# Triangular inverses of the third mixer: from elementwise steps with trips through DRAM to products of 32x32 blocks

## The chip, the core and the metric

The kernel runs on one core of a Trainium2 chip. The metric is the time of one execution on the device, in microseconds (us). TensorE (PE in the rows, PEld for its weight loads) multiplies matrices into PSUM, VectorE (DVE), ScalarE (ACT) and GpSimd (POOL) work elementwise, and SyncE (SP) holds the queue in which nearly all transfers of this kernel are issued. Each engine works through its own instructions in the order of the program and waits on semaphores for the others.

## What is computed

A two-layer diffusion backbone over 512 latent and 256 context tokens of 1024 features. Each layer: a modulated norm, one wide input projection, three token mixers (A: gated linear attention, B: windowed attention, C: bidirectional RWKV-7), a gated merge, and a feed-forward block. The change is in mixer C. Its recurrence, for each of 8 heads of 64 values and for both directions, is

```
def step(S, inp):
    w_t, k_t, v_t, kk_t, a_t = inp[:5]
    sa = jnp.einsum('bhvk,bhk->bhv', S, kk_t)
    S = S * w_t[:, :, None, :] - sa[..., None] * (kk_t * a_t)[:, :, None, :] + v_t[..., None] * k_t[:, :, None, :]
    ...
    return S, jnp.einsum('bhvk,bhk->bhv', S, inp[5])
```

The kernel does it in chunks of 32 tokens. Inside a chunk the tokens' updates depend on one another through a strictly triangular 32x32 matrix L, and T = (I + L)^-1 turns that into one product. For 128 tokens of one direction there are 32 such matrices (4 chunks of 8 heads).

## The kernel before

Mixer C (class Rwkv) takes the 768 tokens in six pieces of 128, in each of two directions, "f" and "b": 12 pieces in a layer, 24 in all. For each piece two steps go ahead of the recurrence, together called a front here. `prep` loads decays (cp), replacement vectors and keys (bk) and keys with queries (kr), and makes the scores X (products xp) and transposed keys bkt (products tp). `inverse` makes TT, the 32 inverses. Then `chain` goes through the piece's four chunks, one after the other, since each needs the state S (sblkf, sblkb) that the last one left. A chunk is a row of short products with a copy behind each: yp, its copy ysb on ACT, up (which reads TT), its copies uv on DVE and ACT, sp, and a sum on DVE into S; op and its copy ys make the output. A tail per piece follows (norm, gate).

`run` moves one lane for each direction in turn, a step at a time. While the chain of one piece goes on, two steps of the next front are written between two steps of the chain (`lane`). In layer 0 one front stands ahead of the chain, in layer 1 two. Between the steps `layer` puts projection jobs of other work (24 in a layer: products px of 512 columns and, in layer 0, pz of 256, each with weights raw that ACT and DVE split into wh and wl). In layer 0 the jobs are spread evenly over the steps; in layer 1 `paced` lets 150 products go first and then 3.3 for each product group of the chain. A scheduler then sets the final order on each engine. The PSUM tiles of xp, tp and of the tail have one tag, "a", with two buffers.

Before the change `inverse` works in a layout of its own, where each of the 32 matrices lies along the free axis of four partitions. X goes to DRAM (d1), comes back as L, spread over four partitions each; G starts as the identity, loaded from the input gid; then 31 steps of a product (L1532, into ftmp) and a subtraction (L1533, into G) solve for the inverse, on DVE for "f" and on POOL for "b"; G goes to DRAM (d2) and comes back as TT. That is 62 elementwise instructions and six transfers for a front. `inverse` yields five times, so a front has ten steps.

## Time and profile before

| what | us |
|---|---|
| median of three runs | 3357.53 (3356.67 to 3370.26) |
| profiled execution: span from first to last instruction | 3361.6 |
| stage of mixer C in layer 0 (first decays scanned at 650.9, last state product at 1159) | about 509 |
| stage of mixer C in layer 1 (2397.4 to 2867.9) | about 471 |
| TensorE busy, whole span | 3033.8 (90%) |

The page gives no time of the profiled execution beside its span. The span is 4 us over the median of the runs, so differences that are worked out against it carry over as they are. Starts and windows are counted from the span's start. [...]

### The profile page before, as it was taken

The page shows a single profiled execution, that of the slowest core. Times are in us where ns is not written, and L with a number is a line of the kernel's source. Part 1 is how long each engine was busy: PE and PEld are TensorE (multiplying, and loading weights), DVE is VectorE, ACT ScalarE, POOL GpSimd, SP SyncE. Part 2 cuts the span into 40 slices and gives each one's busy share as a digit, 9 for nine tenths or more (in the row PEclk, how much of TensorE's full clock was granted, in tenths as well). Part 3 has the DMA queues.
Part 4 walks back from the last instruction along what each step waited for, and adds up shares of the span by engine and source line. Part 5 has one row for each costly group of instructions (what it writes and reads, how often), then busy time and mean ns, then how long its engine had stood idle before and what let it go on. Part 6 is the DMA issues. An engine that isn't in the chain of part 4 may idle for free. (4 is left out here: it accounts for less than half of the span.)

```text
span 3361.6 us, 62705 instructions
## 1 busy us (share of the span) xinstructions
PE 3033.8 (90%) x25760; PEld 2400.0 (71%) x25760; DVE 1756.6 (52%) x3506; ACT 1081.2 (32%) x2034; POOL 990.4 (29%) x1438
## 2 busy tenths in 40 slices
PE   6999999878889989999999899698857789799998
PEld 3777877666666778888888787576635466788887
DVE  3175557766656755222223454656567566643335
ACT  3255444422222233212122344453322222332223
POOL 2033122344655322101001211312266465221102
PEclk9999999888888999999999899798868679899999
DMA  7421222544345552443212322123633444512223
GB/s 289 153 74 56 96 101 95 174 131 124 99 119 142 168 197 73 153 157 132 63 63 95 96 73 95 58 76 126 205 103 107 112 131 137 187 69 95 96 98 119
DMA packets 269375, 398.33 MB, mean 118 GB/s; under 512 B 94624, under 2 KB 179360, under 8 KB 269088
## 3 DMA queue, kind: packets, MB, share of 16 engines
q1 hardware_dynamic: 249184, 370.20, 34.2%
q10 hardware_dynamic: 19904, 24.12, 2.0%
q8 instruction: 202, 3.31, 0.4%
q14 instruction: 85, 0.70, 0.1%
HBM read 320.33 MB, written 73.92 MB: 117 GB/s over the span
## 5 line engine op out<-in xcount | busy, mean ns | idle before, releaser
L50 PE MATMUL px<-hh,wl 128*128 128x512 f32 x1584 | 646.5, 408 | 31.9 <-DVE wl L72 31.8
L50 PE MATMUL px<-hh,wh 128*128 128x512 f32 x1584 | 651.9, 412 | 14.1 <-ACT wh L71 6.5
L50 PE MATMUL px<-hl,wh 128*128 128x512 f32 x1584 | 643.2, 406 | 11.6 <-POOL hl L302 8.8
L72 DVE TENSOR_TENSOR wl<-raw,wh 128x1024 fp32r<-128x1024 f32 (+1 forms) x314 | 402.3, 1282 | 366.4 <-ACT wh L71 332.1
L71 ACT ACTIVATE wh<-raw 128x1024 fp32r<-128x1024 f32 (+1 forms) x314 | 326.1, 1041 | 778.8 <-PE pz L50 395.2
L50 PEld LDWEIGHTS px<-hh,wl 128*128 128x128 f32 x1584 | 308.2, 195 | 110.0 <-DVE wl L72 38.1
L50 PEld LDWEIGHTS px<-hh,wh 128*128 128x128 f32 x1584 | 309.4, 195 | 106.7 <-issue 24.4
L50 PEld LDWEIGHTS px<-hl,wh 128*128 128x128 f32 x1584 | 308.8, 195 | 82.3 <-POOL hl L302 13.2
L673 POOL TENSOR_TENSOR al<-fs,ah 128x768 fp32r<-128x768 f32 (+1 forms) x44 | 85.0, 1931 | 726.3 <-ACT ah L672 726.3
L50 PE MATMUL pz<-hl,wh 128*128 128x256 f32 x872 | 253.1, 291 | 3.8 <-DVE hl L304 2.0
L50 PE MATMUL pz<-hh,wh 128*128 128x256 f32 x872 | 253.5, 292 | 1.5 <-DVE fs L663 1.4
L50 PE MATMUL pz<-hh,wl 128*128 128x256 f32 x872 | 252.0, 289 | 1.3 <-DVE wl L72 0.8
L50 PEld LDWEIGHTS pz<-hl,wh 128*128 128x128 f32 x872 | 171.2, 196 | 10.4 <-POOL hl L302 2.6
L50 PEld LDWEIGHTS pz<-hh,wh 128*128 128x128 f32 x872 | 170.3, 196 | 11.2 <-issue 3.2
L50 PE MATMUL px<-y,wh 128*128 128x512 f32 (+1 forms) x512 | 155.8, 391 | 24.8 <-ACT y L123 10.0
L50 PEld LDWEIGHTS pz<-hh,wl 128*128 128x128 f32 x872 | 170.4, 195 | 7.0 <-issue 5.2
L1532 POOL TENSOR_TENSOR ftmp<-G,L 128x60 f32<-128x60 f32 (+24 forms) x372 | 125.9, 338 | 146.9 <-DMA G<-gid 55.8
L1532 DVE TENSOR_TENSOR ftmp<-G,L 128x60 f32<-128x60 f32 (+24 forms) x372 | 107.4, 289 | 103.8 <-DMA G<-gid 55.6
L1533 POOL TENSOR_TENSOR G<-G,ftmp 128x60 f32<-128x60 f32 (+24 forms) x372 | 131.4, 353 | 25.2
L50 PE MATMUL sp<-uv,bkt 64*64 64x64 f32 x1536 | 99.8, 249 | 36.9 <-DVE uv L1593 36.5
L50 PEld LDWEIGHTS px<-y,wh 128*128 128x128 f32 x512 | 96.1, 209 | 44.2 <-ACT y L123 12.5
L50 PEld LDWEIGHTS sp<-uv,bkt 64*64 64x64 f32 x1536 | 69.3, 147 | 75.4 <-DVE uv L1593 41.1
(443 smaller groups left out, 6090.9 us busy)
## 6 DMA issues: line engine op xcount, KB each, us to landing
raw<-win SPq DMA_DIRECT2D x114, 512.0 KB
raw<-w SPq DMA_DIRECT2D x104, 512.0 KB
araw<-wada SPq DMA_DIRECT2D x96, 512.0 KB
raw<-w SPq DMA_DIRECT2D x48, 448.0 KB
kr<-krd SPq DMA_DIRECT2D x24, 512.0 KB
L<-d SPq DMA_DIRECT2D x24, 512.0 KB
gs<-gat ACTq DMA_DIRECT2D x24, 384.0 KB
raw<-wab SPq DMA_DIRECT2D x16, 512.0 KB
```

The source lines that it names most:

```text
L50: return self.nc.tensor.matmul(out, lhsT=lhsT, rhs=rhs, start=start, stop=stop)
L71: nc.scalar.activation(h[:, :n], raw[:, :n], AF.Copy)
L72: nc.vector.tensor_tensor(out=lo[:, :n], in0=raw[:, :n], in1=h[:, :n].bitcast(F32), op=ALU.subtract)
L673: nc.gpsimd.tensor_tensor(out=al, in0=s, in1=ah.bitcast(F32), op=ALU.subtract)
L1532: eng.tensor_tensor(out=t, in0=G[:, rows, j:j + 1].to_broadcast([128, a, m]), in1=L[:, j:j + 1, cols].to_broadcast([128, a, m]), op=ALU.mult)
L1533: eng.tensor_tensor(out=G[:, rows, cols], in0=G[:, rows, cols], in1=t, op=ALU.subtract)
```

## The change

`inverse` stays in the layout of X. Products with the identity take the blocks out of X twice, as they are and transposed, each block to a 32x32 place of its own (tile iu: rows 32 p for head pair p). VT holds two things per matrix, side by side: the inverse so far and its transpose, beginning with blocks of two rows, I minus the masked part of L. Then four rounds double the block size, 2 to 4 to 8 to 16 to 32: Um is the part of L that joins two blocks (a mask product on POOL), pp = Um times the inverse (tile ip), copied to Ps on ACT, and dd = the inverse times that (tile id, for both halves of VT, in the last round for one), which DVE subtracts from VT, in the last round into TT. All transfers of `inverse` go. It yields ten times now, so a front has fifteen steps. Two constants, imask and eye32, are loaded in place of gid. The PSUM tiles iu, ip and id have the tag "a" too. Comments and docstrings are left out of the changed file, which shifts its line numbers.

```diff
         self.masks = ld("rmask", [128, 2, 64], I["rmask"])
+        self.imask = ld("imask", [128, 5, 32], I["imask"])
+        self.eye = ld("eye32", [128, 32], I["eye32"])
...
     def inverse(self, d, g):
-        """T = (I + L)^-1 of 32 blocks (4 chunks x 8 heads), four partitions per block (row mod 4)"""
-        nc, T = self.nc, self.T
-        d1 = self.D.tile([2, 16, 32, 32], F32, name="d1", tag="d1", bufs=3)   # q, (e w p), j, i
-        d2 = self.D.tile([8, 4, 32, 32], F32, name="d2", tag="d2", bufs=3)    # (q e w), p, j, i
+
+
+        nc, K, T, ps = self.nc, self.K, self.T, self.ps
+        MM = nc.tensor.matmul
         X = self.hs[d, g]["X"]
+        R = (slice(0, 32), slice(96, 128))
+        P = [slice(32 * p, 32 * p + 32) for p in range(4)]
+
+        src = [ps.tile([128, 2, 4, 32], F32, name="iu", tag="a", bufs=2) for _ in range(2)]
+        for p in range(4):
+            for e in range(2):
+                for w in range(2):
+                    for q in range(2):
+                        K.mm(src[q][P[p], 0, 2 * e + w, :], X[R[q], e, w, p, 0:32], K.ident[R[q], R[q]])
+        for p in range(4):
+            for q in range(2):
+                K.mm(src[q][P[p], 1].rearrange("r (e w) i -> r e w i", w=2), K.ident[R[q], R[q]], X[R[q], :, :, p, 0:32])
+        VT = T.tile([128, 2, 8, 32], F32, name="VT", tag="VT", bufs=2)
+        Uc = T.tile([128, 8, 32], F32, name="Uc", tag="Uc", bufs=2)
         for q in range(2):
-            r0 = 0 if q == 0 else 96
-            nc.sync.dma_start(d1[q].rearrange("u j i -> j u i"), X[r0:r0 + 32].rearrange("j e w p i -> j (e w p) i")[:, :, 0:32])
-        L = T.tile([128, 32, 32], F32, name="L", tag="L", bufs=2)
-        nc.sync.dma_start(L.rearrange("u j i -> u (j i)"), d1.rearrange("q u j i -> (q u) (j i)").unsqueeze(0).to_broadcast([4, 32, 1024]))
+            b = slice(4 * q, 4 * q + 4)
+            nc.vector.tensor_tensor(out=VT[:, :, b, :], in0=src[q], in1=self.imask[:, 0:1, :].unsqueeze(1).to_broadcast([128, 2, 4, 32]), op=ALU.mult)
+            nc.scalar.copy(Uc[:, b, :], src[q][:, 1])
         yield
-        G = T.tile([128, 8, 32], F32, name="G", tag="G", bufs=2)
-        nc.sync.dma_start(G, self.I["gid"])
-        tmp = T.tile([128, 128], F32, name="ftmp", tag="ftmp", bufs=2)
-        eng = nc.vector if d == "f" else nc.gpsimd
-        for n in range(31):
-            if d == "f":
-                j, rows, cols = n, slice(0, n // 4 + 1), slice(n + 1, 32)
+        flat = VT.rearrange("r t m i -> r (t m) i")
+        nc.gpsimd.tensor_tensor(out=flat, in0=self.eye.unsqueeze(1).to_broadcast([128, 16, 32]), in1=flat, op=ALU.subtract)
+        def part(n):
+            Um = T.tile([128, 8, 32], F32, name="Um", tag="Um" + d, bufs=1)
+            nc.gpsimd.tensor_tensor(out=Um, in0=Uc, in1=self.imask[:, n + 1:n + 2, :].to_broadcast([128, 8, 32]), op=ALU.mult)
+            return Um
+        Um = part(0)
+        yield
+        for n in range(4):
+            last = n == 3
+            pp = ps.tile([128, 8, 32], F32, name="ip", tag="a", bufs=2)
+            for m in range(8):
+                for r in P:
+                    K.mm(pp[r, m, :], Um[r, m, :], VT[r, 0, m, :])
+            Ps = T.tile([128, 8, 32], F32, name="Ps", tag="Ps", bufs=2)
+            nc.scalar.copy(Ps, pp)
+            if not last:
+                Um = part(n + 1)
+            yield
+            dd = ps.tile([128, 2, 8, 32], F32, name="id", tag="a", bufs=2)
+            for m in range(8):
+                for t in (1,) if last else (0, 1):
+                    for r in P:
+                        lw, rh = (Ps, VT[:, 1]) if t else (VT[:, 1], Ps)
+                        K.mm(dd[r, t, m, :], lw[r, m, :], rh[r, m, :])
+            if last:
+                TT = self.hs[d, g]["TT"] = T.tile([128, 8, 32], F32, name="TT", tag="TT", bufs=4 if self.zout else 6)
+                nc.vector.tensor_tensor(out=TT, in0=VT[:, 1], in1=dd[:, 1], op=ALU.subtract)
             else:
-                j = 31 - n
-                rows, cols = slice(j // 4, 8), slice(0, j)
-            a, m = rows.stop - rows.start, cols.stop - cols.start
-            t = tmp[:, 0:a * m].rearrange("q (a b) -> q a b", b=m)
-            eng.tensor_tensor(out=t, in0=G[:, rows, j:j + 1].to_broadcast([128, a, m]), in1=L[:, j:j + 1, cols].to_broadcast([128, a, m]), op=ALU.mult)
-            eng.tensor_tensor(out=G[:, rows, cols], in0=G[:, rows, cols], in1=t, op=ALU.subtract)
-            if n % 8 == 7:
-                yield
-        nc.sync.dma_start(d2.rearrange("m p (a s) i -> s (m p) a i", s=4), G)
-        TT = self.hs[d, g]["TT"] = T.tile([128, 8, 32], F32, name="TT", tag="TT", bufs=4 if self.zout else 6)
-        nc.sync.dma_start(TT, d2.rearrange("m p r i -> (p r) m i"))
-        yield
+                nc.vector.tensor_tensor(out=flat, in0=flat, in1=dd.rearrange("r t m i -> r (t m) i"), op=ALU.subtract)
+            yield
...
-    g = np.zeros((128, 8, 32), f)
-    for s_ in range(4):
-        for a in range(8):
-            g[32 * s_:32 * s_ + 32, a, 4 * a + s_] = 1
-    C["gid"] = g
...
+    r_, c_ = (p % 32)[:, None], np.arange(32)[None, :]
+    C["imask"] = np.stack([((r_ // (2 * n) == c_ // (2 * n)) & (r_ // n != c_ // n)).astype(f) for n in (1, 2, 4, 8, 16)], 1)
+    C["eye32"] = (r_ == c_).astype(f)
```

How the instructions stand on the engines, at three places. First DVE, layer 0, in the midst of a chain. Before, the steps of an inverse (ftmp, G) stand between the chain's copies uv and state sums sblkb, and the first of them waits for a load:

```order
L1533 TENSOR_TENSOR G<-G,ftmp 128x8x2
L1532 TENSOR_TENSOR ftmp<-G,L 128x8
L1533 TENSOR_TENSOR G<-G,ftmp 128x8
L1606 TENSOR_TENSOR sblkb<-sp,scb 64x4x64 x2
L1532 TENSOR_TENSOR ftmp<-G,L 128x31
L1533 TENSOR_TENSOR G<-G,ftmp 128x31
L1593 COPY uv<-up 32x128
L1532 TENSOR_TENSOR ftmp<-G,L 128x30
L1533 TENSOR_TENSOR G<-G,ftmp 128x30
L1593 COPY uv<-up 32x128
```

Now, at a like place, the round's subtractions (VT from id) stand between the same kinds of chain instruction:

```order
L1564 TENSOR_TENSOR VT<-VT,id 128x512
L1619 COPY uv<-up 32x128 x2
L1632 TENSOR_TENSOR sblkb<-sp,scb 64x4x64 x2
L1475 COPY pc<-cp 128x16
L1564 TENSOR_TENSOR VT<-VT,id 128x512 x3
L1619 COPY uv<-up 32x128
L72 TENSOR_TENSOR wl<-raw,wh 128x1024
L1619 COPY uv<-up 32x128
```

Sixty-two short instructions that hang on two loads have become two masked copies, three subtractions and one last one, which hang on TensorE. Second, TensorE, layer 0, in the midst of a chain. Before, projection products stand between the chain's groups:

```order
L1584 MATMUL up<-ysb,TT 32x64 x3
L1564 MATMUL yp<-uv,X 32x64 x8
L50 MATMUL px<-hh_131,wh 128x512
L50 MATMUL px<-hl_139,wh 128x512
L50 MATMUL pz<-hh_131,wh 128x256
L50 MATMUL pz<-hl_139,wh 128x256
L1590 MATMUL op<-sblkb,kr 32x128 x4
L50 MATMUL px<-hh_131,wl 128x512
```

Now rounds of the next front's inverse stand there as well (ip of 32 products, id of 64, of which the first two rows are shown; a product here is one of the program, and each float32 product of these short ones shows as two MATMUL rows in the profile):

```order
L1610 MATMUL up<-ysb,TT 32x64 x5
L1616 MATMUL op<-sblkb,kr 32x128 x4
L1590 MATMUL yp<-uv,X 32x64 x8
L1595 MATMUL yp<-sblkf,kr 32x128 x4
L50 MATMUL px<-hh_134,wh 128x512
L50 MATMUL ip<-VT,Um 32x32 x32
L50 MATMUL sp<-uv,bkt 64x64 x8
L1637 MATMUL op<-uv,X 32x64 x8
L50 MATMUL id<-Ps,VT 32x32 x4
L50 MATMUL id<-VT,Ps 32x32 x4
```

The chain's sp and op have moved behind a group of 32 inverse products, and the id that needs ScalarE's copy of ip follows after 16 short products. Third, SP's queue in layer 0. Before, the transfers of the inverses (d, L, G, TT) stand between the loads of prep (bk, cp, kr), the chain's values (uv) and the weights (raw):

```order
L1516 DMA d_7183<-X 32x16x32 x2
L1518 DMA L<-d_7148 128x1x1024
L1536 DMA d_6578<-G 4x256x32
L1460 DMA bk<-bkdf_3850 128x4x256
L66 DMA raw<-win 128x1024
L1460 DMA bk<-bkdb_3851 128x4x256
L1538 DMA TT<-d_6578 128x8x32
L1521 DMA G<-gid 128x256
L1518 DMA L<-d_7183 128x1x1024
L1536 DMA d_6584<-G 4x256x32
```

Now the same place holds only the others:

```order
L1462 DMA bk<-bkdf_3850 128x4x256
L66 DMA raw<-win 128x1024
L1462 DMA bk<-bkdb_3851 128x4x256
L1579 DMA uv<-vtok_3854 64x512 x2
L66 DMA raw<-win 128x1024
L1461 DMA cp<-twdb_3849 128x4x136
L1463 DMA kr<-krd_3847 128x4x256
```

No load or store of a front waits in SP's queue for an engine's result any more.

## Rows read from the trace of the kernel before

**Rows 1.** The page: busy time by engine; granted clock in 40 slices.
```profile
PE 3033.8 (90%) x25760; PEld 2400.0 (71%) x25760; DVE 1756.6 (52%) x3506; ACT 1081.2 (32%) x2034; POOL 990.4 (29%) x1438
...
PEclk9999999888888999999999899798868679899999
```
**Rows 2.** Windows: length, PE, PEld, DVE, ACT, POOL busy, PEclk, DMA share, GB/s.
```profile
650.00:740.00 90.00, 73.30 (x708) 60.11 (x706) 55.71 (x108) 26.09 (x44) 42.02 (x88) 0.89 0.60 175
740.00:1079.00 339.00, 292.14 (x4097) 212.25 (x4094) 206.55 (x566) 84.49 (x218) 183.47 (x409) 0.85 0.43 120
1079.00:1159.00 80.00, 78.67 (x1043) 59.34 (x1043) 53.05 (x110) 18.08 (x50) 34.38 (x43) 0.98 0.42 129
2397.00:2505.00 108.00, 68.60 (x649) 51.51 (x648) 56.08 (x120) 26.23 (x42) 47.70 (x90) 0.75 0.56 161
2505.00:2743.00 238.00, 186.17 (x2392) 123.86 (x2390) 153.14 (x415) 56.66 (x138) 142.33 (x329) 0.74 0.43 117
2743.00:2868.00 125.00, 124.34 (x1880) 83.35 (x1881) 76.95 (x193) 32.49 (x97) 61.99 (x114) 0.90 0.39 122
```
**Rows 3.** Waits of PE, 650 to 1159: total us, times, longest.
```profile
PE sp L50 <- DVE uv L1593: 31.6, 7, 8.7
PE px L50 <- DVE wl L72: 11.6, 9, 6.7
```
**Rows 4.** Waits of PE, 2397 to 2868: total us, times, longest.
```profile
PE up L1584 <- DMA TT<-d: 27.4, 4, 16.2
PE px L50 <- DVE wl L72: 19.0, 7, 10.8
PE xp L50 <- POOL kr L1479: 11.9, 2, 7.3
```
**Rows 5.** DVE groups, 650 to 1159: busy, mean ns | idle before, releasers.
```profile
L1532 DVE TENSOR_TENSOR ftmp<-G,L 128x60 f32<-128x60 f32 (+24 forms) x186 | 54.1, 291 | 46.1 <-DMA L<-d 23.0 <-DMA G<-gid 12.6 <-issue 5.7
L1533 DVE TENSOR_TENSOR G<-G,ftmp 128x60 f32<-128x60 f32 (+24 forms) x186 | 53.5, 288 | 5.1
```
**Rows 6.** Timeline of DVE near 2502: start, us, what, [idle before <-releaser].
```profile
2502.33 0.19 DVE L1532 TENSOR_TENSOR ftmp<-G,L 128x31 f32<-128x31 f32 x1 [21.02 <-DMA G<-gid]
...
2503.11 0.27 DVE L1593 COPY uv<-up 32x128 f32<-32x128 f32 x1
```
**Rows 7.** The page's groups: inverse steps on both engines, and the product reading TT.
```profile
L1532 POOL TENSOR_TENSOR ftmp<-G,L 128x60 f32<-128x60 f32 (+24 forms) x372 | 125.9, 338 | 146.9 <-DMA G<-gid 55.8
L1532 DVE TENSOR_TENSOR ftmp<-G,L 128x60 f32<-128x60 f32 (+24 forms) x372 | 107.4, 289 | 103.8 <-DMA G<-gid 55.6
...
L1584 PE MATMUL up<-ysb,TT 32*32 32x64 f32 x1536 | 55.7, 245 | 36.1 <-DMA TT<-d 31.0 <-ACT ysb L1574 5.0
```
**Rows 8.** Timeline of PE near 205.7, mixer A: short products in a dense run.
```profile
205.75 1.02 PE L50 MATMUL gsc<-gD,gD 64*32 64x32 f32 x96
206.71 0.87 PE L880 MATMUL gktp<-ident,gkh 128*128 128x128 f32 x6
```
**Rows 9.** Timeline of PE near 519.4: products that all write one column strip.
```profile
519.41 1.68 PE L1412 MATMUL pb<-rksel,kt 128*32 128x2 f32 x48
521.02 0.65 PE L1143 MATMUL sop<-sPT,svt 128*64 128x256 f32 x4
```
**Rows 10.** Timeline of PE near 859.4: 128-column products into four strips.
```profile
859.42 0.43 PE L1590 MATMUL op<-sblkb,kr 128*32 128x128 f32 x8
859.77 0.68 PE L50 MATMUL sp<-uv,bkt 64*64 64x64 f32 x16
```
**Rows 11.** Timeline of PE near 2861, the same form at the lower clock.
```profile
2861.12 0.66 PE L1569 MATMUL yp<-sblkb,kr 128*32 128x128 f32 x8
2861.71 1.18 PE L1584 MATMUL up<-ysb,TT 32*32 32x64 f32 x32
```
**Rows 12.** Windows, columns as in group 2: the end of layer 1's chain.
```profile
2857.50:2868.00 10.50, 10.11 (x184) 6.33 (x167) 4.95 (x12) 2.41 (x10) 2.46 (x4) 0.50 0.14 44
```
**Rows 13.** Instructions on X: the masked copy, duration ns min/median/max.
```profile
L1492 DVE TENSOR_TENSOR X<-xp,rmask x48: 406/680/692, 665.9 to 2728.3; 128x512 f32<-128x512 f32 x40, 128x256 f32<-128x256 f32 x8
```

## The prediction, made before the changed kernel ran

> **What bounds the kernel now.** I read the page first. TensorE is busy for 90% of the span, and its granted clock dips in two stretches, around slices 8 to 14 and 29 to 34 [rows 1]. Those are the two stages of mixer C, so the windows come next [rows 2]. The stage of layer 0 is 509 us long (90 + 339 + 80) with TensorE busy for 444.1, so it idles 64.9; that of layer 1 is 471 us with 379.1 busy and 91.9 idle. DVE and POOL are below 70% in each. What the reader is to see: in these stages TensorE is the fullest engine, what is left to gain are 157 us of its idle time and the time lost to the lower clock, and work added to it has no other place to go. The clock share, weighted by length, is (90 x 0.89 + 339 x 0.85 + 80 x 0.98) / 509 = 0.88 in layer 0 and (108 x 0.75 + 238 x 0.74 + 125 x 0.90) / 471 = 0.785 in layer 1. [...]

> Then the waits of TensorE. In layer 0 half of the idle time is sp waiting for DVE's copy uv, 31.6 us in 7 waits, and 11.6 are for split weights wl [rows 3]. In layer 1 it is up waiting for TT, 27.4, then wl, 19.0, and the scores waiting for POOL's kr, 11.9 [rows 4]. The groups of DVE say why a copy of 0.27 us is late by up to 8.7: the first step of an inverse stands in DVE's order and waits for its loads, 23.0 us for L and 12.6 for G in layer 0 alone [rows 5]; the timeline shows one such wait of 21.02 us with the copies uv behind it [rows 6]. So the old inverse hurts less by its 62 instructions than by blocking two engines on transfers.

> **What goes.** 24 fronts x 31 steps x 2 instructions. In layer 0 DVE loses 54.1 + 53.5 = 107.6 us of its 315 [rows 2, 5], and gains per front two masked copies and a last subtraction at half size, 0.406 each, and three at full size, 0.680 [rows 13]: 3.3 us x 12 = 39. POOL loses more than that (its product step alone is 125.9 in the whole kernel [rows 7]) and gains five operations for each front. ACT gains six copies. None of the three was the bound and all end with room, so this ledger itself is worth nothing; what counts is that their blocking waits go. Six transfers for each front leave SP's queue too.

> **What TensorE gets.** Per front iu is 32 products of 32 columns and 8 of 128, ip 4 x 32, id 3 x 64 + 32: 392 in all. A float32 product shows as two rows (up: 24 fronts x 4 chunks x 8 = 768 products, 1536 rows [rows 7]), so 784 rows.

> - ip and id are 256 + 448 = 704 rows of 32x32 blocks on the diagonal of the array, in groups of 64 or 128. Their nearest row is mixer A's gsc: 96 rows, 32 columns each, until the next group starts 0.96 us later [rows 8], 10.0 ns each, with the turn to another shape in it: 7.0 us.
> - The 64 short rows of iu write one column strip for 16 rows on end, from two row strips in turn. pb writes one strip with all its rows: 48 in 1.61 us, 33.5 ns each [rows 9]. I take half, since two strips alternate: 1.1 us.
> - The 16 long rows: op's 8 rows of 128 columns go to four strips in 0.35 us, 44 ns each [rows 10]; with two strips twice that, 1.4 us.

> That is 9.5 us for a front, 114 for a stage, 228 in all, at full clock. At the lower one the same 8 rows take 0.59 us instead of 0.35, 69% more [rows 10, 11]. The bounds: 784 x 10.0 ns = 7.8 us a front below, 784 x 33.5 = 26.3 above, if nothing overlaps. I take the low end because the long groups are like gsc's, dense and on separate strips.

> [...]

> **What comes back.** Of the idle time, in layer 0 the waits for uv and a part of wl (45 of 64.9), in layer 1 those for TT, kr and most of wl, with what queued behind them (70 of 91.9). Against that stand new waits. A front passes between TensorE and another engine nine times, and an id stands behind ACT's copy of its ip, a subtraction before the next ip. Such a copy is 0.4 to 0.7 us by DVE's rows [rows 13]; behind a waiting id stand the chain's next products and the projections. Bare, 24 x 8 of them at 0.55 would be 106 us; in the order shown, other products stand between nearly always, so I take 15. Net return 100 us (157 to 57).

> The clock: idle stretches are where it falls, but not only they. At the end of layer 1's chain TensorE is busy for 10.11 of 10.50 us with short products alone, and the granted clock is 0.50 [rows 12]. The inverse's products are of this kind, so the clock gains only part of what the shorter waits promise: I take 0.88 to 0.90 in layer 0 and 0.785 to 0.865 in layer 1. On the old work that is 444 x (1 - 0.88 / 0.90) = 10 and 379 x (1 - 0.785 / 0.865) = 35, together 45 us back. The lower level is then left for 20% and 27%, which costs the new products 114 x 0.69 x 0.20 = 16 and 114 x 0.69 x 0.27 = 21.

> **The sum.** 228 + 16 + 21 - 100 - 45 = +120 us, against the profiled 3361.6: 3482. The median of the runs is 4 us under that execution, so 3477 us, 3.6% slower. By layer: 0 pays 114 + 16 - 40 - 10 = +80, and 1 pays 114 + 21 - 60 - 35 = +40. With 100 to 190 us coming back in place of 145, this case gives 3430 to 3525.

> A change below 0.5% (17 us) I call no change, since a measurement of this kernel tells little more.

> **Rivals.**

> - *Little comes back*, chance 0.14. The short bursts take the place of the idle time as the cause of the low clock, and each also delays the chain's next product, since TensorE takes them in order. [...] Against it: DVE's blocking waits go in any case. Price with the clock as now: 228 + 114 x 0.69 x (0.24 + 0.43) = 281, less 45 of idle: +236, 3594 us.
> - *It pays for itself*, chance 0.08. 265 us of price and as much returned: 3340 to 3375. For it: in the last 125 us of layer 1, with the inverses nearly done, TensorE is busy for 124.34 [rows 2], so its idle time is the fronts' doing. It needs nearly all idle time and half of the clock's loss.
> - *The waits were the real price: faster*, chance 0.07. All idle time (157) and full clock on the old work (444 x 0.12 + 379 x 0.215 = 135) would be 292 us, against 228 at full clock. It turns faster by over 0.5% when more than 245 of the 292 come back; with nine tenths, 3361.6 + 228 - 263 = 3327, by the median 3323 us. For it: the stage of layer 1 is a chain of waits, not of work, for its first 346 us (254.8 busy [rows 2]). Against it: the low clock of short products [rows 12], and layer 0, which has little to return.
> - *The blocks don't overlap*, chance 0.05. If products of ip and id, which share PSUM banks from different row strips, go one after the other as pb's do, a front costs 26.3 us and the kernel 631 more; with 100 back about 3890 us. For it: nothing in the trace has this diagonal form in a long run. Against it: gsc [rows 8]. [...]

> **How the numbers follow.** The forecast has the remaining 0.66. Predicted: 3477. The range reaches down to 3395, where the clock gives twice what I took and a little more idle time goes, and up to 3600, which takes in the case in which little comes back; left out are the two cases with less loss or a gain (0.15) and the serial one (0.05). Slower by over 0.5%: 0.66 + 0.14 + 0.05 = 0.85; within: 0.08; faster: 0.07.

> **What would show it.** Groups iu, ip and id of some 18,800 rows, ip and id at about 10 ns of busy time for each row, and iu below 3 us a front; if they stand at 20 or more, the price is wrong. No wait of DVE or POOL for a load of an inverse, and sp <- uv in layer 0 below 10 us; if it stays near 30, the blocking wasn't the cause. Stages of about 590 and 510 us: if layer 1's gets shorter than 471, the waits were worth more than I took, and if its PEclk is below 0.78, the clock is the reason for a larger loss. TensorE waiting for Ps (ACT) or VT (DVE) for more than 30 us in a stage would say that the round trips are bare.

## The result, and the profile after

The changed kernel takes 3660.73 us (median of four runs, 3658.18 to 3665.66) against 3362.56 for the kernel before beside it (3356.67 to 3370.26): ratio 1.088, 95% interval 1.086 to 1.091. The direction was forecast, the size was not: +298 us where I had +120, and outside the range that ended at 3600.

The profiled execution spans 3660.1 us. Its page: busy time by engine with the number of instructions (for PE, of product rows), the granted clock in 40 slices, and the queue whose packets the page calls instructions.

```profile
PE 3281.9 (90%) x44576; PEld 2645.8 (72%) x44576; DVE 1643.3 (45%) x2906; ACT 1125.5 (31%) x2178; POOL 848.4 (23%) x814
...
PEclk9999999877777889999999899898767778899999
...
q8 instruction: 349, 5.72, 0.6%
```

The same queue on the page before (packets, MB, share of 16 engines):

```profile
q8 instruction: 202, 3.31, 0.4%
```

TensorE's share is 90% as in [rows 1], which says nothing: the span grew with the work. Two other lines do. The clock dips deeper and longer than in [rows 1]. (PEclk is a share of full speed. Its record in the traces of both kernels has two levels, 1.00 and 0.50; a mean between them says that a part of the stretch was at the lower one.) And 18,816 more rows, each with its weight load 37,632 more instructions, came with 147 more packets of program: 256 instructions or 128 rows for each, 16.4 KB. (The queue is TensorE's own, as far as counts can say: 349 packets of 256 are 89,344 instructions, and TensorE has 2 x 44,576 = 89,152. In the kernel before it is 202 x 256 = 51,712 against 2 x 25,760 = 51,520.)

The two stages of mixer C, in the columns of [rows 2]:

```profile
644.10:1302.60 658.50, 573.96 (x15286) 456.42 (x15288) 261.39 (x483) 150.37 (x385) 194.53 (x228) 0.81 0.27 85
2544.80:3160.90 616.10, 502.76 (x14334) 383.15 (x14334) 228.57 (x428) 137.53 (x348) 178.57 (x220) 0.76 0.25 79
```

They are 658.5 and 616.1 us long, where they were 509 and 471: +295, so the whole loss is here. Idle time rose from 157 to 85 + 113 = 198, and the clock fell from 0.88 and 0.785 to 0.81 and 0.76. Both were to move the other way. What waits now, in layer 0:

```profile
PE id L50 <- issue: 50.7, 30, 3.0
PE sp L50 <- DVE uv L1619: 6.2, 6, 3.3
```

and in layer 1:

```profile
PE id L50 <- issue: 61.8, 34, 2.7
PE ip L50 <- issue: 12.5, 9, 2.0
```

The old waits went as foretold: sp for uv from 31.6 us [rows 3] to 6.2, up for TT from 27.4 [rows 4] to nothing. In their place stand waits of id for "issue": the trace knows no semaphore and no engine that they end with. The groups (busy, mean ns | idle before, releasers) say that nearly all idle time before ip and id is of this kind, and that the round trips I had priced (Ps from ACT, Um from POOL, VT from DVE) are small:

```profile
L50 PE MATMUL id<-VT,Ps 32*32 32x32 f32 x6144 | 151.0, 216 | 64.0 <-issue 63.9
L50 PE MATMUL id<-Ps,VT 32*32 32x32 f32 x4608 | 122.0, 216 | 49.4 <-issue 48.7 <-ACT Ps L1550 0.6
L50 PE MATMUL ip<-VT,Um 32*32 32x32 f32 x6144 | 89.1, 213 | 18.9 <-issue 14.8 <-POOL Um L1539 1.9 <-ACT cp L1469 1.4
```

The timeline of PE shows where such a wait lies: inside a group whose operands are all there.

```profile
787.69 0.24 PE L50 MATMUL id<-VT,Ps 32*32 32x32 f32 x8
787.75 0.26 PE L50 MATMUL id<-Ps,VT 32*32 32x32 f32 x7
789.81 0.18 PE L50 MATMUL id<-Ps,VT 32*32 32x32 f32 x1 [1.79 <-issue]
789.81 0.26 PE L50 MATMUL id<-VT,Ps 32*32 32x32 f32 x8
```

I call an idle time of over 0.3 us between two rows of one group a **gap**, for iu, ip and id and for the chain's short products yp, up and op. The changed kernel has 93 in its two stages, 159.6 us; the one before has one, of 0.4 us. Seven of the 93, 9 us, end with a copy, mask or sum of another engine. The other 86 lie multiples of 128 rows apart (to four rows), the content of one packet of program.

The trace also holds the packets of program. In the two stages TensorE has 94 idle times of over 0.3 us that end with "issue", in any group, 156 us in all. Every one of them ends 1.2 to 1.7 us after such a packet has landed; the moments at that distance from a landing are only 9% of the two stages.

### The profile page after: what moved, and what is told of

Read it like the earlier page. It is cut to its first block, busy times and chain, and to the rows that moved or that the text cites. A ratio compares the mean times of both kernels' runs of the same rounds, so it can differ in the third digit from the quotient of the medians.

```text
span 3660.1 us, 99249 instructions
## 1 busy us (share of the span) xinstructions
PE 3281.9 (90%) x44576; PEld 2645.8 (72%) x44576; DVE 1643.3 (45%) x2906; ACT 1125.5 (31%) x2178; POOL 848.4 (23%) x814
## 5 line engine op out<-in xcount | busy, mean ns | idle before, releaser
L50 PEld LDWEIGHTS px<-hh,wh 128*128 128x128 f32 x1584 | 311.1, 196 | 112.1 <-issue 27.1
L50 PE MATMUL id<-VT,Ps 32*32 32x32 f32 x6144 | 151.0, 216 | 64.0 <-issue 63.9
L50 PEld LDWEIGHTS id<-VT,Ps 32*32 32x32 f32 x6144 | 132.3, 128 | 73.9 <-issue 72.5
L1564 DVE TENSOR_TENSOR VT<-VT,id 128x512 f32<-128x512 f32 x72 | 49.5, 688 | 272.7 <-PE id L50 272.6
L50 PE MATMUL id<-Ps,VT 32*32 32x32 f32 x4608 | 122.0, 216 | 49.4 <-issue 48.7
L50 PEld LDWEIGHTS id<-Ps,VT 32*32 32x32 f32 x4608 | 108.7, 128 | 55.5 <-issue 53.8
```

The lines of the kernel that those rows point to most:

```text
L50: return self.nc.tensor.matmul(out, lhsT=lhsT, rhs=rhs, start=start, stop=stop)
L1564: nc.vector.tensor_tensor(out=flat, in0=flat, in1=dd.rearrange("r t m i -> r (t m) i"), op=ALU.subtract)
```

## The experiments

Theory 1: TensorE runs out of instructions. Rival 1: the gaps are hidden round trips or waits for tiles. Rival 2: the clock is what costs. The table is for reading along: time of a kernel, and from its trace, for both stages together, TensorE's busy time (each row counted until the next one starts) in iu, ip and id and in all other products, the gaps, and the idle time beside them. (In e2, 12 of the 50 us of gaps end with another engine; in the other versions of both directions it is 9 us or less.)

| kernel | us | iu, ip, id | gaps | other idle | other products |
|---|---|---|---|---|---|
| before (profiled execution) | 3362 | - | 0.4 | 156 | 823 |
| changed | 3661 | 261 | 160 | 38 | 816 |
| e6: no inverse | 3173 | - | 0.4 | 32 | 752 |
| e2: bfloat16 | 3394 | 125 | 50 | 43 | 794 |
| e5: wide products added | 3656 | 402 | 74 | 40 | 750 |
| e7: 64 columns | 3633 | 322 | 115 | 48 | 760 |
| e8: up to 128 columns | 3661 | 456 | 30 | 58 | 731 |
| c4: bfloat16, 64 columns | 3383 | 134 | 37 | 46 | 775 |
| c5: c4, wide moves | 3383 | 113 | 40 | 49 | 791 |

Where no interval is given, a time is that of one run; eleven runs of the kernel before, taken beside e8, spread over 17 us (3347 to 3364).

**e1, the products by themselves.** Behind the last product of the kernel before:

```diff
+        self.probe()
...
+                for m in range(count // 4):
+                    c = n * (m % (512 // n))
+                    for r in P:
+                        put(self.mm(t[r, c:c + n], src[r, r], src[r, 0:n]))
```

`probe` multiplies identity blocks, in a fixed order, and no operand is written meanwhile.

> The kernel before, and behind its last product runs of products that wait for nothing (identity blocks into a scratch bank, four row strips in turn): 1024 rows of 32 columns in float32, 512 rows of 32 columns in bfloat16, 512 rows of 64 and 512 of 128 columns, and 16 times 64 rows of 32 columns with four wide products between. Theory 1 (TensorE runs out of instructions: a piece of its program holds 128 such rows and the next one comes only every 3.2 to 3.8 us): the run of 1024 rows shows gaps of 1 to 3 us, about 128 rows apart, and takes 20 to 30 us instead of the 10 us that 10 ns a row give; so does the one in bfloat16 (10 to 15 us instead of 5); fewer or no gaps where 128 rows take longer, and none in the last sequence. Rival 1 (the gaps are waits for tiles or for the round trip to ScalarE and VectorE): no gap above 0.3 us anywhere in these runs, 1024 rows in 10 us. Rival 2 (clock): no gaps, 1024 rows in 10 us, or 20 us with every row twice as long.

Timeline of PE; pa has 32 columns, pc 64, pd 128, pe 32 in short runs:

```profile
3352.74 1.47 PE L50 MATMUL pa<-ident 32*32 32x32 f32 x150
3356.14 1.29 PE L50 MATMUL pa<-ident 32*32 32x32 f32 x128 [1.94 <-issue]
3359.89 1.93 PE L50 MATMUL pa<-ident 32*32 32x32 f32 x128 [2.46 <-issue]
3363.36 1.93 PE L50 MATMUL pa<-ident 32*32 32x32 f32 x128 [1.54 <-issue]
3366.83 1.93 PE L50 MATMUL pa<-ident 32*32 32x32 f32 x128 [1.54 <-issue]
...
3410.53 1.99 PE L50 MATMUL pc<-ident 32*32 32x64 f32 x128 [1.75 <-issue]
3414.01 1.99 PE L50 MATMUL pc<-ident 32*32 32x64 f32 x128 [1.49 <-issue]
...
3424.88 14.18 PE L50 MATMUL pd<-ident 32*32 32x128 f32 x512
...
3442.62 0.75 PE L50 MATMUL pe<-ident 32*32 32x32 f32 x64
```

1024 rows took 26.2 us with seven gaps, each 128 rows after the last. From start to start such a piece takes 3.47 us (3359.89 to 3363.36), with rows of 32 columns as with 64 (3410.53 to 3414.01, 3.48): the time is the piece's, not the row's. (The first full piece took 3.75.) The packets show what the 3.47 us are made of: a packet's transfer starts 1.1 us after the first row of a piece, takes 0.9 to 1.3 us, and the next piece goes on 1.3 to 1.5 us after it has landed. Rows of 128 columns take 14.18 / 512 = 27.7 ns, 3.55 us for 128 of them, and show no gap; 64 rows between wide products show none either. The run in bfloat16 took 9.2 us with two gaps, a little less than I had expected. No other engine is at work and no tile is waited for, so rival 1 is out for these runs. The windows of pa, the bfloat16 run, pc and the mixed run (columns of [rows 2], the clock before the last two):

```profile
3352.74:3378.90 26.16, 14.06 (x1026) 13.11 (x1025) 0.00 (x0) 0.00 (x0) 0.00 (x0) 0.61 0.02 4
...
3387.64:3396.80 9.16, 4.63 (x514) 4.40 (x513) 0.00 (x0) 0.00 (x0) 0.00 (x0) 0.77 0.02 5
3405.13:3417.80 12.67, 7.94 (x513) 7.40 (x512) 0.00 (x0) 0.00 (x0) 0.00 (x0) 1.00 0.02 4
...
3442.60:3511.00 68.40, 67.38 (x1149) 32.51 (x1148) 0.00 (x0) 0.00 (x0) 0.00 (x0) 1.00 0.01 2
```

Both runs of 32 columns spent part of their time at the lower level (0.61 and 0.77 in the mean); the run of 64 columns, with its gaps, did not (1.00).

**e6, no inverse at all.** TT is a copy of the identity, so the inversion is left out.

```diff
-        src = [ps.tile([128, 2, 4, 32], F32, name="iu", tag="a", bufs=2) for _ in range(2)]
...
+        nc.gpsimd.tensor_copy(TT, self.eye.unsqueeze(1).to_broadcast([128, 8, 32]))
```

> The changed kernel without the inverse: its products, copies and masks are left out, and TT is a copy of the identity; the steps of the order stay. What before minus this gives is the whole return that taking the elementwise steps and their loads away can bring; after minus this is the whole price of the products. Theory 1: the return is some 100 us (idle time of 157 us less some 55), so 3240 to 3280 us, and the price some 390 us, of which 261 are busy rows and the rest gaps that go with them. Rival 1 the same return. Rival 2 (clock): also the clock comes back here, 3150 to 3230 us.

```profile
651.00:1074.90 423.90, 409.02 (x5883) 314.30 (x5884) 226.69 (x414) 127.04 (x312) 150.70 (x176) 0.95 0.40 132
2314.80:2674.70 359.90, 342.61 (x4924) 237.80 (x4926) 187.05 (x356) 114.87 (x276) 131.20 (x168) 0.89 0.41 132
```

3172.89 us. The return is 185 us, not 100: idle time falls by 124 and, as rival 2 had it, the clock comes back too (0.95 and 0.89), 71 us on the other products. (That is 195 in the two stages; the rest of the kernel gives some of it back.) The full price of TensorE's inverse is then 488 us: 261 of rows, 160 of gaps, 6 of other idle time, and 64 that the other products lose by the lower clock (491 together).

**e2, half the instructions.** The tiles of the inverse in bfloat16 (values rounded), one row for each product.

```diff
-        VT = T.tile([128, 2, 8, 32], F32, name="VT", tag="VT", bufs=2)
+        VT = T.tile([128, 2, 8, 32], BF16, name="VT", tag="VT", bufs=2)
```

and the same for Uc, Um and Ps.

> The changed kernel with the tiles of the inverse (VT, Uc, Um, Ps) in bfloat16, so that each product of ip and id is one row instead of two; their values are rounded, the round trips, tiles and order stay. 352 rows a front in place of 704 (iu stays at 80). Theory 1: the program shrinks with the rows, so the gaps of 160 us fall to 50 us or less, and with the 100 us of work saved the time falls by 190 us or more, to below 3475 us. Rival 1 (round trips): the gaps stay near 160 us, only the work goes, 3550 to 3570 us. Rival 2 (clock): the time follows the share at the lower clock, gaps stay.

```profile
L50 PE MATMUL id<-VT,Ps 32*32 32x32 bf16 x3072 | 61.6, 181 | 11.3 <-issue 11.0 <-ACT Ps L1550 0.3
L50 PE MATMUL ip<-VT,Um 32*32 32x32 bf16 x3072 | 42.1, 178 | 29.2 <-issue 16.0 <-POOL Um L1539 8.1 <-DVE VT L1564 3.8
```

3394.39 us: 266 less, of which 136 are rows, 110 gaps and 22 the other products, while the round trips are as many as before. Theory 1's bounds held.

**e5, work added.** Three wide products in the middle of each group of id, into places that are written over or read by nobody.

```diff
+                if m == 4:
+                    for _ in range(3):
+                        K.mm(dd[:, :, 4:8, :].rearrange("r t m i -> r t (m i)"), K.ident, K.ident.unsqueeze(1).to_broadcast([128, 2, 128]))
```

> The changed kernel with work added: in the middle of each group of id, three products of 256 columns (identity blocks, into the half of the bank that the group writes next, so nothing new is waited for). 96 groups by six rows of 0.23 us (half of the 0.46 us that a row of 512 columns took in the run of dense products) are 133 us of added work at the full clock. Theory 1 (pieces of the program come every 3.5 us or so): a piece that holds fillers lasts longer, so most of the added time falls into gaps that were there anyway: the gaps fall from 160 us to 60 us or less and the time rises by at most 50 us, to below 3710 us, or falls. Rival 1 (round trips): the gaps stay and the time rises by 110 us or more, to above 3770 us. Rival 2 (clock): the wide products bring the clock back, so the old products of the two stages get faster by 30 us or more, while gaps stay.

```profile
648.10:1292.80 644.70, 598.57 (x15576) 473.04 (x15576) 261.87 (x484) 150.73 (x385) 196.00 (x228) 0.92 0.27 87
2535.30:3155.70 620.40, 553.14 (x14622) 409.96 (x14622) 232.03 (x428) 137.97 (x348) 177.68 (x220) 0.88 0.24 78
```

3655.69 us: 141 us more of busy time in the inverse, and no more time. The gaps fell by 86, to 74 (I had said 60), and the other products by 66, since the clock is at 0.92 and 0.88, where the changed kernel had 0.81 and 0.76: rival 2's share is real, not much smaller than the gaps'.

**e7 and e8, wider rows, same instructions.** Each product takes more blocks of columns than it needs; the next ones write over the rest.

```diff
-                        K.mm(dd[r, t, m, :], lw[r, m, :], rh[r, m, :])
+                        K.mm(dd[r, t, m:min(m + 2, 8), :], lw[r, m, :], rh[r, m:min(m + 2, 8), :])
```

and for ip alike; e8 has 4 in place of 2.

> The changed kernel with the same instructions, but each product of ip and id (but the last of eight) takes two blocks of columns, 64 in place of 32; the second half is written over by the next product, so the values are the same. In the runs of dense products a row of 64 columns took 15.5 ns and one of 32 columns 9.8 ns at the full clock, so 16,896 rows, seven eighths of them wider, are 84 us more of busy time. Theory 1 (a piece of 128 rows comes every 3.5 us, however long its rows are): the added time falls into the gaps, which lose 60 us or more of their 160, and the time stays within 30 us of 3660 us, or falls. Rival 1 (round trips, or rows as the only price): the gaps stay and the time rises by 80 us or more, to 3740 us or above. Rival 2 (clock): in the dense runs of 64 columns the granted clock stayed at 1.00, in those of 32 columns it fell to 0.61; if that holds here, the clock is back, the old products of the two stages take some 60 us less and the time falls to 3550 to 3620 us.

> The changed kernel with up to four blocks of columns for each product of ip and id (128 columns, 96, 64 and 32 for the last three of eight), the same instructions and values. By the dense runs (27.7 ns a row of 128 columns, 15.5 of 64, 9.8 of 32) a row takes 23 ns on average and 128 rows 3.0 us, near the 3.5 us in which a piece of the program comes: 16,896 rows are 392 us of busy time where the changed kernel showed 220. Theory 1: 172 us more work take the place of gaps, which fall from 160 to 25 us or less; with the clock's return of some 60 us the time is 3590 to 3680 us. Rival 1 (round trips, rows as the only price): 3800 us or more, gaps as before. Rival 2 (clock): the same clock as with two blocks, its return alone 60 us: 3770 us.

Groups of e8, then its two stages:

```profile
L50 PE MATMUL id<-VT,Ps 32*32 32x128 f32 (+3 forms) x6144 | 254.0, 252 | 11.2 <-issue 10.2 <-PE ip L50 0.2
L50 PE MATMUL id<-Ps,VT 32*32 32x128 f32 (+3 forms) x4608 | 213.8, 250 | 5.3 <-issue 5.0
```

```profile
650.70:1333.00 682.30, 641.56 (x15288) 535.59 (x15288) 264.12 (x483) 150.68 (x385) 190.67 (x228) 0.92 0.26 82
2572.00:3165.20 593.20, 546.00 (x14332) 440.75 (x14334) 229.20 (x428) 137.47 (x348) 180.13 (x220) 0.95 0.26 82
```

3633.46 us with 64 columns, 3660.76 with up to 128. In e8 ip and id are busy for 416 us instead of 220, and the time lies within the spread of the changed kernel's runs (3658 to 3666): the gaps fell from 160 to 30, which is two thirds of what was added, and the clock (0.92 and 0.95) gave back 85 on the other products, less 20 of other idle time. Rival 1 had these at 3740 and 3800 or more; rival 2, without the gaps, had e8 at 3770. In e7 theory 1's gaps were to lose 60 and lost 45, and rival 2's 3550 to 3620 us was not reached, though the clock came back (0.89 and 0.90, 57 us on the other products).

**e4, loads further ahead in the kernel before.**

```diff
-        yield
         G = T.tile([128, 8, 32], F32, name="G", tag="G", bufs=2)
         nc.sync.dma_start(G, self.I["gid"])
+        for _ in range(5):
+            yield
```

> The kernel before, with its elementwise inverse, but the loads of L and G issued together and five more steps of the order between them and the first elementwise step, so that VectorE and GpSimd don't stand waiting for them in front of the copies that the chain needs. Theory 1's reading of the kernel before (the wait for these loads blocks VectorE, so that TensorE waits before sp in layer 0 and before up in layer 1): those two waits, 31.6 and 32.4 us, fall below 15 us each and the time falls by 20 to 60 us, to 3300 to 3340 us. If those waits are something else: within 10 us of 3360.

3379.03 us, ratio 1.006 (1.004 to 1.008): a miss. DVE's waits in layer 0:

```profile
DVE ftmp L1533 <- DMA L<-d: 19.6, 3, 11.4
DVE ftmp L1533 <- DMA G<-gid: 15.1, 2, 13.7
```

and TensorE's:

```profile
PE sp L50 <- DVE uv L1594: 23.9, 5, 9.6
```

The first two were 23.0 and 12.6 [rows 5], the third 31.6 [rows 3]; up's wait for TT in layer 1 went from 27.4 to 25.6. So neither of TensorE's waits fell below 15. Five steps more between load and use hardly moved where the scheduler put them: from the issue of the first L to its first use it is 12.6 us in both kernels. So this run doesn't test what the waits cost. e6 does, which takes them away.

**e3, e3b and c2, one direction each way.** The forward inverse on TensorE (float32; bfloat16; bfloat16 with its masks on VectorE), the backward one elementwise on GpSimd as before. All three also give each tile of either inverse one buffer in place of two, apart from Um, which had one.

```diff
-            yield from self.inverse(d, g)
+            yield from (self.inverse if d == "f" else self.inverse_e)(d, g)
```

> TensorE's inverse for the forward direction alone, the elementwise one on GpSimd for the backward direction: half of the products (130 us). Theory 1: the bursts of two directions no longer stand together, so that the gaps fall to less than half of 160 us, 30 to 70 us; VectorE has no elementwise steps and no loads to wait for, which gives back more than half of what taking all of them away gave (185 us): 3172 + 130 + 50 + 30 to 60 for GpSimd's waits, 3390 to 3450 us. Rival 1 (round trips of the inverse): half of everything, 3510 us with some 80 us of gaps. Rival 2 (clock): also 3510 us, the lower clock over half of the added time.

> The same with the tiles of the forward inverse in bfloat16 (values rounded), one row for each of its products. Theory 1: products 62 us, gaps 10 to 20 us, and the same return, so 3300 to 3350 us: below the kernel before. Rivals 1 and 2: half way between the kernel before and the one with both directions in bfloat16 (3394 us), 3375 us.

> The inverse of the forward direction by TensorE with bfloat16 tiles, its masks and its first difference on VectorE instead of GpSimd; the elementwise one of the backward direction stays on GpSimd. If the waits for GpSimd's masks, which stood behind its elementwise steps, made the mixed version slow (3462 us; 23 us of TensorE's waits name Um), they go: 3400 to 3440 us by those waits alone, and 3300 to 3350 us if they also held up the chain. If the backward direction's own elementwise steps on GpSimd are what is waited for: 3450 us or more.

3570.28, 3462.36 (ratio 1.031, 1.028 to 1.034) and 3483.18 us: e3 and e3b are worse than any of the theories had them, and c2 is in its last case (3450 or more), in which the backward direction's own steps on GpSimd are what is waited for. The gaps behaved (29, 18 and 5 us), but other idle time rose to 208, 179 and 181 us, more than before the change. Waits of PE in e3b:

```profile
PE tp L1506 <- POOL bk L1500: 26.4, 14, 13.9
```

and in c2, where the masks no longer stand on GpSimd:

```profile
PE tp L1506 <- POOL bk L1500: 49.5, 16, 13.6
```

A step of GpSimd ahead of the chain is late, behind the elementwise steps that it kept. Why it is later than in the kernel before, which had them too, I did not follow; the single buffers weren't tested by themselves.

**c4 and c5, a version that might beat both.** c4 is e2 with e7's wider rows. c5 also copies X's blocks to a bfloat16 tile Xc, so that eight products of 128 columns of weights do what 32 did:

```diff
-                        K.mm(src[q][P[p], 0, 2 * e + w, :], X[R[q], e, w, p, 0:32], K.ident[R[q], R[q]])
+                    K.mm(src[q][:, 0, 2 * e + w, :], Xc[R[q], e, w].rearrange("r p i -> r (p i)"), self.idb[R[q], R[q]])
```

> Both: the inverse in bfloat16 and 64 columns for each product of ip and id. With one row for each product there are 50 us of gaps to fill and 8,448 rows to widen, 42 us. Theory 1: within 15 us of the 3394 us of the version in bfloat16 alone. Rival 1: 3435 us. Rival 2 (clock): if the wider rows hold the clock up, 3340 to 3370 us.

> The version in bfloat16 with two blocks of columns (3383 us), and the blocks of X copied to a bfloat16 tile without gaps between them by GpSimd, so that eight products of 128 columns of weights give the transposed blocks in place of 32 products of 32, and each is one row: iu has 16 rows a front where it had 80, the inverse 368 where it had 432. iu took 37 us in both stages; by rows like them it takes 15 to 20 us. Theory 1: a sixth less of program, so 5 to 10 us of the 37 us of gaps go as well: 3350 to 3365 us, level with the kernel before or a little below. Rival 1: only the rows go, and the copy on GpSimd is one more step to wait for: 3365 to 3390 us.

c4: 3382.69 us, 12 below e2, in theory 1's bounds; a difference of that size lies within the spread of single runs. c5: 3382.78 us, ratio 1.009 (1.007 to 1.011). iu fell to 15 us as expected, and the time did not: the gaps stayed at 40 and the other products took 15 us more. So theory 1's 3350 to 3365 us was missed, and rival 1's 3365 to 3390, in which only the rows go, held. No version beat the kernel before; these two come within 1%.

## Why the prediction was wrong

**What TensorE gets** was right in its sum: 10.9 us a front with the lower clock in it (261 / 24), against 228 + 16 + 21 = 265 us in all. ip and id stand on separate strips, and rows like theirs ran at 9.8 ns in e1, as gsc had suggested [rows 8]. That the sum fits so well is in part luck. iu took 1.7 us a front where I had 2.5, and ip and id 13.0 ns a row where I had 10.0: by the trace's record of the clock 49% of them (8,213 of 16,896 rows) started at the lower level, where I had 20 and 27%. With 9.8 ns a row in e1's first piece and 15.1 in its later ones (1.93 us for 128 rows; 0.61 in the mean over the run) I estimate 12.4 of the 13.0 ns from that. The shares of time at the lower level in my sums follow from the mean clock and a lower level of 0.50 [rows 12]. The 20 and 27% go with the 0.90 and 0.865 that I expected, and the run doesn't show them: the record has 38 and 49% of the two stages at 0.50. For the kernel before, 0.24 and 0.43 in the price of the rival "little comes back" go with 0.88 and 0.785, and its record has 25 and 44%.

**What goes** was right: the blocking waits of DVE and POOL are gone, and sp and up no longer wait (above).

**What comes back** is the step that failed, in both of its terms. The net return of idle time was to be 100 us (157 to 57); idle time rose to 198 instead. The return itself was there: without gaps 38 us are left, 19 better than forecast. But of "new waits" I had only round trips, 15 us; what came were 160 us of gaps, in 150 of which TensorE had no instructions. The clock was to rise to 0.90 and 0.865 and give 45 us on the old work; it fell to 0.81 and 0.76, and the old work got back 7. That idle stretches are where the clock falls, but not only they, is what the traces have as well: in the two stages of the kernel before TensorE is busy for 79 and 71% of the time at 0.50 and for 90 and 88% of the time at 1.00; in those of the changed kernel it is 86 and 79% against 88 and 84%. The sum by measured terms: 261 - 7 + 41 = +295. Of the 175 us between this and my +120, the gaps are 160 and the clock 38, less 19 of other idle time and 4 of rows. My sign for the clock (below 0.78 in layer 1) came, and named the smaller of the two causes.

The gaps are the price of instructions, shown from four sides: they end as a packet of program has landed (94 of the 94 that no engine ends); alone, with no other engine, they come every 128 rows and 3.47 us (e1); with half the instructions and the same round trips they fall to a third (e2); and with the same instructions and rows nearly twice as long they all but go, with no time added that the runs could tell (e8). A packet holds 256 instructions (37,632 more instructions came with 147 more packets). Its arrival shows as no gap in e1's 512 rows of 128 columns (14.18 us), and as seven in its 1024 rows of 32 (26.2 us), where a row takes 9.8 to 15.1 ns within a piece and the mean over a full piece is 3.47 / 128 = 27.1 ns.

**The rival "little comes back"** (3594 us) had the clock right, in kind: with the inverse on TensorE it is lower (0.81 and 0.76, without it 0.95 and 0.89 in e6). It lacked the gaps. Whether the narrow rows or the gaps between them pull the clock down is not settled: e5, e7 and e8 changed both, and so do e1's runs. Two comparisons speak for the rows. [rows 12] has the lower level for 10.5 us in which TensorE is busy for 10.11. And of e2 (32 columns, 50 us of gaps) and e7 (64 columns, 115 us of gaps) the one with fewer gaps has the lower clock; layer 1 of each:

```profile
2421.30:2899.00 477.70, 427.84 (x10110) 314.25 (x10110) 228.79 (x428) 136.96 (x348) 171.33 (x220) 0.80 0.31 100
2545.10:3134.50 589.40, 496.37 (x14332) 385.78 (x14334) 227.87 (x428) 136.32 (x348) 175.38 (x220) 0.90 0.26 82
```

## What to carry to other kernels

Count instructions as well as busy time when work moves to TensorE: a short float32 product is two rows here, each with a weight load (PE and PEld x44576 each), and 128 such rows (256 instructions) came no faster than every 3.5 us in e1. So the short products cost 27 ns a row there in a long run (3.47 us for 128), and 10.6 ns in runs of 64 with wide products between them, which give the program time to arrive (0.68 us from 3442.62 to 3443.30, no gap). Look for idle time that ends with "issue" inside a group whose operands are ready. If the instructions can't be made fewer (bfloat16 halved them), try longer rows or other work within the groups, which were nearly free up to that time here: 141 us more of busy time in e5, 61 in e7 and 196 in e8 gave 3655.7, 3633.5 and 3660.8 us, where the changed kernel takes 3660.7. They raised the clock as well, from 0.81 and 0.76 to 0.92 and 0.88 (e5), 0.89 and 0.90 (e7), 0.92 and 0.95 (e8).
